# Four edits to the schedule of a one-core decoder block: first loads, two staging tiles, one unit's order of steps, one epilogue

## The chip, the cores and the metric

The kernel runs on one core of one Trainium2 chip. The metric is the device time of one execution, in microseconds (us). A core has a tensor engine for matmuls (PE; its loading of the standing operand is listed as PEld), a vector engine (DVE), a scalar engine (ACT), GpSimd (POOL) and a sync engine (SP). The engines run side by side, each takes its own instructions in order, and they wait for one another through semaphores. SP and POOL are used here mainly to issue transfers (DMAs) between DRAM and the on-chip memory.

## What is computed

The block takes x (256 tokens, 4096 channels, float32), normalises it, and projects it to 20480 channels. Half-width parts of that feed two branches; both branches go back to full width, are weighted by sigmoid gates and added, pass an output matrix, and the result is added to x and normalised again. Cut to what matters:

```
h    = rmsnorm(x, norm_w)
proj = h @ w_in                                   # (256, 20480)
u_p, z_p, u_c, b_c, c_c, z_c, g = split(proj)     # six parts of 2048, one of 8192
y_pool = pool(u_p, pool_w, pool_scale) * silu(z_p)
y_conv = b_c * conv3(c_c * u_c) * silu(z_c)
br     = [y_pool @ w_branch[0], y_conv @ w_branch[1]]
merged = sum over n of sigmoid(g[n] + gate_b[n]) * br[n]
out    = rmsnorm(x + merged @ w_out, final_norm_w)
```

## The kernel before

**Units and steps.** All the large products are cut into *units* of 1024 output columns for all 256 tokens. The units run in this order: `cu0, cc0, cz0, cb0, cu1, cc1, cz1, cb1` (the convolution branch, L583 to L620), `pz0, pu0, pz1, pu1` (pooling), eight gate units `g0_0, g1_0, ... g1_3`, then `b0_0, b1_0, b0_1, ... b1_3` (the branch products), and `o0` to `o3` (the output matrix). A unit is a row of *steps*; one step multiplies 256 channels of the left operand with a 256 x 1024 block of weights and adds into PSUM banks. A unit has 16 steps (branch units 8, whose left operand has 2048 channels).

**Two kinds of step.** Every float32 operand is split into a high and a low part in a reduced format, and three products of parts stand for one. A plain step, P, is 24 matmuls of 128x512. A Strassen step, S, is 21 matmuls (seven products of three) but needs sums of the weight blocks first: `sums`, `direct`, `t13` and `t24` (L264 to L287). ACT writes the high parts (`act`, L68) and DVE makes sums and low parts (`add` and `sub`, both L71), from the tile `raw`, where the weights land, to the tile `ring`, from which PE reads. Each S step also uses four PSUM banks called shared, in which the epilogue of the unit before does its transposes.

**What sets the order.** The program is written out in one static order by a small planner. `pump` (L1073) prepares weights up to AHEAD = 3 steps in front of PE, as far as the `ring` of 60 slots has room (a P step takes 16, an S step 28), and issues the next weight load as soon as one of NRAW = 3 slots of `raw` is prepared (L1076). `tick` (L1110) runs once per 6 matmuls: it takes one item from the epilogue's queue of the unit before, and calls `pop_fill`. In `after_group` (L1128) the emptying of finished PSUM banks comes first, then the ticks, then the limit is moved and `pump` runs. So an epilogue is a list of items, one per tick, in which `gap(n)` stands for n empty ticks. Where the S steps of a unit stand is given by a sequence: `seq_even` puts them at 2, 4, 6, 8, 10, 12, 14, `seq_turned` (L571, `spread_sequence(NS_X, 5)`) at 5, 7, 8, 10, 11, 12, 14. Unit `cu1` uses `seq_turned`, and so does `pz0`.

**Left operands.** The first 20 units use the parts of x, held in the tile `arena`. The branch units use y, kept in DRAM (`y_d`), and the output units use the merged result (`m_d`). When the last gate unit `g1_3` begins, `queue_fills` (L1147) lists all these operands in the order of their use as *fills*: eight for branch 0, eight for branch 1, two more for each branch's last unit (`y_last`, the same channels in the plain form, which go to the slots of the operands that they replace), and those of m. `pop_fill` (L837) looks at each tick at that list. At most one fill is done per PACE = 5 ticks: ACT and DVE split a staged operand into `arena`, if it was fetched at least LANDING = 6 ticks ago and its slot is free. Then, if one of the two staging tiles (`sa`, upper half, and `sb`) is empty, POOL fetches (`move`, L90) the next operand:

```
used = [f.st for f in fills if f.at is not None]
st = next((q for q in stages if not any(q is u for u in used)), None)
to_come = [f for f in fills if f.at is None and not isinstance(f, Direct) and f.ready()]
if st is not None and to_come:
    nxt = next((f for f in to_come if f.free()), None if used else to_come[0])
```

A fill whose slot is not free can thus be fetched when both stages are empty, and then keeps its stage until the slot is free. `ready` says whether y is there: for branch 0 always, for branch 1 from the start of `b0_0`. A step whose operand is not there yet forces a fill (L1188).

**The first steps.** The very first step is loaded in three pieces, the first 512 columns of each of two halves of the channels and then the other 512 columns, with x's first part in between (L1062 to L1066, SP). `par` (the convolution's taps and bias, 32 KB) is loaded at step 6 of the program by POOL, which has nothing before it and issues at once. While the first steps run, ACT squares x piece by piece (`square`, L949) and DVE adds; after the last piece one fold is left to do in halves, and at step 10 PE sums over the channels with ones (`sum_squares`, L960). The root mean square enters later, when a unit's sums are read out of PSUM by `evacuate` (L416, ACT, tile E or the unit's own target).

**The branch units' epilogue** (L721) in ticks, for branch 1: fetch the gate into E, 7 empty ticks, the product R = R * E, an empty tick, the sum R = R + Y with branch 0's part, 5 empty ticks, the transposes of R on PE (L466) with copies out, and the store to `m_d`.

Of the kernel before, what the change touches and what calls it, by code (L numbers as in the profile page):

```python
# [32 lines left out]
P = 128  # L33
T = 256
# [19 lines left out]


@with_exitstack
def hybrid_block(ctx: ExitStack, tc: tile.TileContext, x, x_t, norm_t, w_in, pool_w, pool_scale,
                 conv_t, gate_b, w_branch, w_out, final_norm_w, out):

# [166 lines left out]
    class Step:  # L226
# [95 lines left out]
        def groups(self):  # L322

            gs = []
            if self in steps[0:2]:

                for n in range(2):

                    order = ((0, 0), (1, 0), (0, 1), (1, 1), (2, 0), (2, 1)) if self is steps[0] and n == 0 else (
                        [(i, k) for i in range(3) for k in range(2)])  # L330
                    for i, k in order:
                            for t in range(2):
                                ah, al = self.op.standing(k, t)
                                h, l = self.h[n][:, k], self.l[n][:, k]
                                gs.append([("E", t, n), [((ah, h), (al, h), (ah, l))[i]], None])
                    gs[-1][2] = [(self.blocks[n], 8)]
            elif self.kind == "P":
                order = [(t, n) for n in self.halves for t in self.toks]
                if self.ending:
                    order = [(t, n) for t in self.toks for n in self.halves]  # L340
                for t, n in order:
                    mm = []
                    for k in range(2):
                        ah, al = self.op.standing(k, t)
                        h, l = self.h[n][:, k], self.l[n][:, k]
                        mm += [(ah, h), (ah, l), (al, h)]
                    gs.append([("E", t, n), mm, None])
                    if self.final and t == self.toks[-1]:
                        gs[-1][2] = [(self.blocks[n], 8)]
            elif self.kind == "S":  # L350
                prods = {"M1": (A11, self.dh, self.dl, 0, ("F", 0, 0)),
                         "N3": (Q3, self.dh, self.dl, 1, ("E", 0, 0)),
                         "M2": (A12, self.dh, self.dl, 2, ("E", 0, 1)),
                         "N5": (Q5, self.h13, self.l13, 0, ("F", 0, 1)),
                         "N7": (Q7, self.h13, self.l13, 1, ("F", 1, 0)),
                         "N6": (Q6, self.h24, self.l24, 0, ("F", 1, 1)),
                         "N4": (A22, self.h24, self.l24, 1, ("E", 1, 1))}
                order = ("N3", "M2", "N4", "M1", "N5", "N7", "N6") if self.closing else (
                    "M1", "N3", "M2", "N5", "N7", "N6", "N4")
# [127 lines left out]
    def gap(n):  # L487
        return [None] * n
# [94 lines left out]
    def conv_units(c, first=False):  # L583
        base = 2 * HALF + c * NU

        def c_epi(u):
            items = gap(1) + [lambda: mul(R, R, Y)] + gap(8)

            def taps(j):
                v, y = bankview(j), chan(Y)  # L590
                for i in range(2):
                    b = 2 * j + i
                    kb = 8 * c + b
                    act(y[:, b], v[:, i], AF.Identity, scale=par[:, 32 + kb:33 + kb], bias=par[:, 48 + kb:49 + kb])
                for i in range(2):
                    b = 2 * j + i
                    kb = 8 * c + b
                    for s in (1, 2):
                        col = 16 * (2 - s) + kb
                        stt(y[:, b, s:], v[:, i, 0:T - s], par[:, col:col + 1], y[:, b, s:], ALU.mult, ALU.add)  # L600

            for f in transposes(R, taps):
                items += [f, None]
            return items

        def gate(j):
            y = chan(Y)[:, 2 * j:2 * j + 2]
            mul(y, bankview(j), y)

        def z_epi(u):  # L610
            return sigmoid_mul() + [lambda: move(z_d[c], R)]

        def b_epi(u):
            return [lambda: move(E, z_d[c])] + gap(6) + [lambda: mul(R, R, E)] + gap(4) + transposes(R, gate) + [
                lambda: put(y_d[1, c], chan(Y))]

        in_unit(f"cu{c}", base, lambda u: [], seq=seq_0 if first else seq_turned, dst=Y)
        in_unit(f"cc{c}", base + 2 * HALF, c_epi, seq=seq_even if c else None)
        in_unit(f"cz{c}", base + 3 * HALF, z_epi)
        in_unit(f"cb{c}", base + HALF, b_epi, seq=seq_even)  # L620
# [99 lines left out]
    def branch_unit(n, c):  # L720
        def epi(u):  # L721
            if n == 0:
                return gap(2) + [lambda: mul(Y, R, Y)]
            items = [lambda: move(E, gates_d[n, c])] + gap(7)

            def copy(j):
                act(chan(Y)[:, 2 * j:2 * j + 2], bankview(j))
            return items + [lambda: mul(R, R, E), None, lambda: add(R, R, Y)] + gap(5) + pairs(
                transposes(R, copy)) + [
                lambda: c < 3 and put(m_d[c], chan(Y)), lambda: merged.update({c: now[0] + (STORED if c < 3 else 0)})]  # L730

        def src(i):
            return wbr[n, c, i]
        direct = c == 3 and n in DIRECT_LAST
        units.append(Unit(f"b{n}_{c}", src, seq_yp if direct else seq_y, y_last[n] if direct else y_ops[n], epi,
                          before=None if n else lambda: move(Y, gates_d[n, c])))
        return units[-1]
# [211 lines left out]
    def square(c):  # L949

        src = xc(2 * c, 2 * c + 2)
        if c == 0:
            act(sq, src, AF.Square)
        else:
            act(flat(V), src, AF.Square)
            add(sq, sq, flat(V))
        if c == 7:
            add(sq[:, 0:2 * T], sq[:, 0:2 * T], sq[:, 2 * T:])

    def sum_squares():  # L960
        for t in range(2):
            for k in range(2):
                pin(nc.tensor.matmul(sums_x[:, t:t + 1], sq[:, k * T + t * P:k * T + (t + 1) * P], ones[:, 0:1],
                                     start=k == 0, stop=k == 1))

    def diagonals():
        for t, q in enumerate((diag, std)):
# [67 lines left out]
    for i, c in squares.items():  # L1035
        after(i, square, c)
    before(6, load_x, 12, 16)
    before(6, move, par, conv_t)
    at(10, sum_squares)
    at(10, rstd)  # L1040
    at(10, diagonals)
# [14 lines left out]
    def issue_load(s):  # L1056
        i = s.load_index
        r = raw[:, i % NRAW]
        if s.kind == "M":
            load(r.rearrange("p (k n) -> p k n", k=4), s.src)  # L1060
        elif i == 0:
            q = r.rearrange("p (k n) -> p k n", k=2)  # L1062
            load(q[:, 0, 0:NH], s.src[:, 0, 0:NH])
            load_x(0, 1)
            load(q[:, 1, 0:NH], s.src[:, 1, 0:NH])
            load(q[:, :, NH:NU], s.src[:, :, NH:NU])  # L1066
        else:
            load(r.rearrange("p (k n) -> p k n", k=2), s.src)
        s.raw = r
# [77 lines left out]
    def queue_fills():  # L1147
# [3 lines left out]
            prev, owner[o.region] = owner[o.region], o  # L1151
            return freed(prev)

        def from_y(n, o, i):
            later(o, y_d[n, i // 4][:, i % 4].rearrange("p k t -> p (k t)"), place_of(o), lambda: n == 0 or units_done[0])

        def from_m(o, i):
            c = i // 4
# [9 lines left out]
                from_y(n, y_ops[n][i], i)  # L1168
        for n in DIRECT_LAST:
            for i in range(NP_Y, ny):  # L1170
                from_y(n, y_last[n][i], i)
        for i in order_of(seq_late):
            from_m(m_ops[i], i)

# [154 lines left out]
def _layout(i):  # L1329
# [3 lines left out]
    def by_step(w, pairs, units):  # L1333
# [4 lines left out]
        "x": i["x"],  # L1338
        "x_t": i["x"][0].T.reshape(D // T, 2, P, T).transpose(2, 0, 1, 3),
        "norm_t": i["norm_w"][0].reshape(-1, P).T,  # L1340
        "w_in": by_step(i["w_in"][0], D // T, -1),
        "pool_w": i["pool_w"][0].reshape(4, 4, P, NH).transpose(0, 2, 1, 3),
        "pool_scale": i["pool_scale"],
# [28 lines left out]
```

## Time and profile before

| | us |
|---|---|
| median of 3 runs | 2400.67 |
| lowest, highest | 2400.47, 2402.05 |
| the profiled execution's own time | 2400.08 |
| its span, from the first instruction to the last | 2398.4 |
| PE busy in it | 2380.3 |
| DVE busy | 2101.8 |
| ACT busy | 1351.6 |

The mean clock that TensorE was granted is 0.998 of full speed. A profile is of one execution, and its times count from its first instruction. In its timelines a row gives start, duration, engine, line of the kernel, operation, what it writes and reads, the count of instructions merged, and in brackets the idle time of the engine before it and what ended that idle time. In the groups by line, the numbers after the bar are the busy time, the mean duration in ns, and after the second bar the idle time before them. Where helpers record every operation, the line is the helper's (L68, L71, L83, L86, L90), and the tile's name tells which work it is. A stored copy of x's norm weights is named `par_n`; the matmuls of all steps are at L1122.

### The profile page before, as it was taken

How to read it: one execution, taken by the hardware profiler on the slowest of the kernel's cores; microseconds unless marked ns; L12 is line 12 of the kernel's file. 1: busy time of each engine (PE TensorE's matmuls, PEld its weight loads, DVE VectorE, ACT ScalarE, POOL GpSimd, SP SyncE). 2: the span in 40 equal slices, each digit the busy share in tenths (PEclk: the TensorE clock that was granted, in tenths of full speed). 3: DMA queues.
4: the chain of work that ended last, by engine and by line, in shares of the span. 5: the costliest groups of instructions: out<-in, count | busy, mean ns of one | idle time of the engine just before them, and what ended most of it. 6: DMA issues, size and time to landing. Idle time of an engine off the chain costs nothing.

```text
span 2398.4 us, 27788 instructions
## 1 busy us (share of the span) xinstructions
PE 2380.3 (99%) x10608; PEld 1970.6 (82%) x10608; DVE 2101.8 (88%) x2094; ACT 1351.6 (56%) x1392; POOL 61.2 (3%) x135
## 2 busy tenths in 40 slices
PE   9999999999999999999999999999999999999998
PEld 7888888888888888888888888888878888888886
DVE  8889989988989868968999899889888886799998
ACT  7555555555556555556555555555564555555564
POOL 0000000000000000000000000000000001000000
PEclk9999999999999999999999999999999999999999
DMA  8455564555566445545666566566666568556657
GB/s 334 167 202 196 224 244 179 211 202 202 212 242 228 187 180 224 219 176 221 236 237 233 214 224 222 212 242 232 254 242 236 214 255 291 207 204 246 249 216 272
DMA packets 79830, 538.73 MB, mean 225 GB/s; under 512 B 9152, under 2 KB 9152, under 8 KB 18512
## 3 DMA queue, kind: packets, MB, share of 16 engines
q1 hardware_dynamic: 68240, 484.47, 54.1%
q0 software_dynamic: 11024, 51.42, 6.3%
q8 instruction: 83, 1.36, 0.2%
q10 hardware_dynamic: 432, 1.07, 0.1%
q14 instruction: 51, 0.42, 0.0%
HBM read 511.75 MB, written 25.17 MB: 224 GB/s over the span
## 4 chain that ended last, share of the span: by engine, by line
PE 97%; DVE 1%; DMA 1%; issue 0%; ACT 0%; SPq 0%; DVEq 0%; ACTq 0%
PE sums L1122 77%; PE shared L1122 18%; PE shared L690 1%; PE shared L466 1%; DMA raw<-in_w_in_dram 1%; DVE ring L71 0%; DMA E<-gates_d 0%; DVE R L71 0%; ACT ring L68 0%; PE shared L669 0%; PE shared L670 0%; PE shared L672 0%; SPq L86 0%; DVE raw L71 0%; DVE V L71 0%
## 5 line engine op out<-in xcount | busy, mean ns | idle before, releaser
L1122 PE MATMUL sums<-ring,arena 128*128 128x512 f32 x8292 | 1942.3, 390 | 5.0 <-ACT arena L68 3.3
L1122 PEld LDWEIGHTS sums<-ring,arena 128*128 128x128 f32 x8292 | 1553.6, 188 | 328.3 <-ACT ring L68 2.5
L68 ACT ACTIVATE ring<-raw 128x1024 fp32r<-128x1024 f32 (+2 forms) x901 | 988.2, 1136 | 744.5 <-PE sums L1122 263.3
L71 DVE TENSOR_TENSOR ring<-raw,ring 128x1024 fp32r<-128x1024 f32 (+2 forms) x901 | 1162.3, 1322 | 216.6 <-ACT ring L68 184.7
L1122 PE MATMUL shared<-ring,arena 128*128 128x512 f32 x1968 | 497.1, 389 | 0.0
L1122 PEld LDWEIGHTS shared<-ring,arena 128*128 128x128 f32 x1968 | 369.5, 188 | 76.6
L68 ACT ACTIVATE ring<-V 128x1024 fp32r<-128x1024 f32 x164 | 173.2, 1056 | 115.4 <-DVE V L71 76.3
L71 DVE TENSOR_TENSOR V<-raw 128x1024 f32<-128x1024 f32 x164 | 199.9, 1219 | 1.4 <-DMA raw<-in_w_out_dram 1.4
L71 DVE TENSOR_TENSOR ring<-V,ring 128x1024 fp32r<-128x1024 f32 x164 | 199.9, 1219 | 0.3 <-ACT ring L68 0.2
L71 DVE TENSOR_TENSOR raw<-raw 128x512 f32<-128x512 f32 x164 | 113.5, 692 | 5.7
L71 DVE TENSOR_TENSOR raw<-V,raw 128x512 f32<-128x512 f32 x164 | 113.4, 691 | 5.1
L71 DVE TENSOR_TENSOR R<-R,E 128x1024 f32<-128x1024 f32 (+1 forms) x55 | 95.1, 1745 | 4.7 <-DMA E<-gates_d 3.7
L68 ACT ACTIVATE E<-sums,rin 128x512 f32<-128x512 f32 (+1 forms) x57 | 44.7, 826 | 30.6 <-PE sums L1122 30.3
L71 DVE TENSOR_TENSOR R<-R,shared 128x512 f32<-128x512 f32 x84 | 57.4, 683 | 1.1
L68 ACT ACTIVATE arena<-sa 128x512 fp32r<-128x512 f32 (+2 forms) x41 | 22.4, 567 | 49.1 <-DVE sa L71 44.0
L71 DVE TENSOR_TENSOR R<-R,Y 128x1024 f32<-128x1024 f32 (+1 forms) x28 | 40.4, 1447 | 0.0
L71 DVE TENSOR_TENSOR arena<-sa,arena 128x512 fp32r<-128x512 f32 (+2 forms) x41 | 24.5, 616 | 11.9 <-ACT arena L68 11.9
L466 PEld LDWEIGHTS shared<-ident,R 128*128 128x128 f32 x160 | 19.3, 140 | 5.4 <-DVE R L71 1.3
L466 PE MATMUL shared<-ident,R 128*128 128x128 f32 x160 | 22.7, 273 | 0.9 <-DVE R L71 0.9
L68 ACT ACTIVATE R<-R 128x2048 f32<-128x2048 f32 x8 | 15.3, 1909 | 14.5 <-DVE R L71 14.5
L690 PE MATMUL shared<-ring 128*128 128x512 f32 x96 | 22.1, 389 | 0.0
L690 PEld LDWEIGHTS shared<-ring 128*128 128x128 f32 x96 | 18.0, 188 | 3.7
(132 smaller groups left out, 402.0 us busy)
## 6 DMA issues: line engine op xcount, KB each, us to landing
raw<-in_w_in_dram SPq DMA_DIRECT2D x319, 1024.0 KB, 4.9
raw<-in_w_branch_dram SPq DMA_DIRECT2D x64, 1024.0 KB, 5.3
raw<-in_w_out_dram SPq DMA_DIRECT2D x64, 1024.0 KB, 4.9
gates_d<-R POOLq DMA_DIRECT2D x8, 1024.0 KB, 5.2
raw<-in_pool_w_dram SPq DMA_DIRECT2D x4, 1024.0 KB, 4.8
Y<-in_gate_b_dram POOLq DMA_DIRECT2D x8, 512.0 KB, 6.9
Y<-gates_d POOLq DMA_DIRECT2D x4, 1024.0 KB, 8.9
E<-gates_d POOLq DMA_DIRECT2D x4, 1024.0 KB, 5.5
```

The costliest lines, as they stand in the source:

```text
L68: return pin(nc.scalar.activation(dst, src, func, **kw))
L71: return pin(nc.vector.tensor_tensor(out=dst, in0=a, in1=b, op=op))
L466: pin(nc.tensor.transpose(shared(j)[:, i * T + t * P:i * T + (t + 1) * P], src[:, t, c:c + P], ident))
L690: pin(nc.tensor.matmul(o, a[:, k, ts], b[:, k], start=(k, i) == (0, 0), stop=(k, i) == (3, 2)))
L1122: pin(nc.tensor.matmul(ps, lhs, rhs, start=n == 0, stop=n == u.total[b] - 1))
```

## The change

Six places are changed.

1. The first step's weights come from an extra input, `w_first`, which holds the same 256 x 1024 block as four pieces of 128 x 512, each contiguous in DRAM. The three loads stay, with the same bytes and targets.
2. `par` is loaded through SP and not through POOL, at the same place of the program.
3. After the last square, DVE folds the sums twice and not once, down to one column per token, and PE's sum over the channels takes two matmuls and not four.
4. `cu1` takes `spread_sequence(NS_X, 4)`: its S steps stand at 4, 6, 7, 9, 11, 12, 14.
5. In branch 1's epilogue the product moves one tick later, to the tick just before the sum. The length of the list is the same.
6. The two extra fills of each branch's last unit count as ready only when all sixteen first operands of both branches have been filled.

```
-            load(q[:, 0, 0:NH], s.src[:, 0, 0:NH])
+            load(q[:, 0, 0:NH], w_first[0, 0])
             load_x(0, 1)
-            load(q[:, 1, 0:NH], s.src[:, 1, 0:NH])
-            load(q[:, :, NH:NU], s.src[:, :, NH:NU])
+            load(q[:, 1, 0:NH], w_first[0, 1])
+            load(q[:, :, NH:NU], w_first[1].rearrange("k p n -> p k n"))
...
+        "w_first": i["w_in"][0][:T, 2 * HALF:2 * HALF + NU].reshape(2, P, 2, NH).transpose(2, 0, 1, 3),
...
-    before(6, move, par, conv_t)
+    before(6, load, par, conv_t)
...
         if c == 7:
-            add(sq[:, 0:2 * T], sq[:, 0:2 * T], sq[:, 2 * T:])
+            for n in (2 * T, T):
+                add(sq[:, 0:n], sq[:, 0:n], sq[:, n:2 * n])
...
         for t in range(2):
-            for k in range(2):
-                pin(nc.tensor.matmul(sums_x[:, t:t + 1], sq[:, k * T + t * P:k * T + (t + 1) * P], ones[:, 0:1],
-                                     start=k == 0, stop=k == 1))
+            pin(nc.tensor.matmul(sums_x[:, t:t + 1], sq[:, t * P:(t + 1) * P], ones[:, 0:1], start=True, stop=True))
...
-        in_unit(f"cu{c}", base, lambda u: [], seq=seq_0 if first else seq_turned, dst=Y)
+        in_unit(f"cu{c}", base, lambda u: [], seq=seq_0 if first else spread_sequence(NS_X, 4), dst=Y)
...
-            items = [lambda: move(E, gates_d[n, c])] + gap(7)
+            items = [lambda: move(E, gates_d[n, c])] + gap(8)
...
-            return items + [lambda: mul(R, R, E), None, lambda: add(R, R, Y)] + gap(5) + pairs(
+            return items + [lambda: mul(R, R, E), lambda: add(R, R, Y)] + gap(5) + pairs(
...
-        def from_y(n, o, i):
-            later(o, y_d[n, i // 4][:, i % 4].rearrange("p k t -> p (k t)"), place_of(o), lambda: n == 0 or units_done[0])
+        def from_y(n, o, i, ready=None):
+            later(o, y_d[n, i // 4][:, i % 4].rearrange("p k t -> p (k t)"), place_of(o),
+                  ready or (lambda: n == 0 or units_done[0]))
...
-                from_y(n, y_last[n][i], i)
+                from_y(n, y_last[n][i], i, lambda: all(o.ready for q in y_ops for o in q))
```

More of the change, by code (lines that the diff above doesn't have):

```diff
@@ L56, in hybrid_block @@
 @with_exitstack
-def hybrid_block(ctx: ExitStack, tc: tile.TileContext, x, x_t, norm_t, w_in, pool_w, pool_scale,
+def hybrid_block(ctx: ExitStack, tc: tile.TileContext, x, x_t, norm_t, w_first, w_in, pool_w, pool_scale,
                  conv_t, gate_b, w_branch, w_out, final_norm_w, out):
@@ L331, in groups @@
                     for i, k in order:
[L332 to L335, printed above, removed]
+                        for t in range(2):
+                            ah, al = self.op.standing(k, t)
+                            h, l = self.h[n][:, k], self.l[n][:, k]
+                            gs.append([("E", t, n), [((ah, h), (al, h), (ah, l))[i]], None])
                     gs[-1][2] = [(self.blocks[n], 8)]
```

## The prediction

> **What bounds the kernel now.** I read the page first: TensorE's share, then who it waited for, then its timeline, since only a hole in TensorE's row can be worth time here.
>
> ```profile
> span 2398.4 us, 27788 instructions
> ...
> PE 2380.3 (99%) x10608; PEld 1970.6 (82%) x10608; DVE 2101.8 (88%) x2094; ACT 1351.6 (56%) x1392; POOL 61.2 (3%) x135
> ...
> L1122 PE MATMUL sums<-ring,arena 128*128 128x512 f32 x8292 | 1942.3, 390 | 5.0 <-ACT arena L68 3.3
> ```
>
> PE is busy for 2380.3 of 2398.4 us. Matmuls are not removed by this change except four tiny ones, so the most that it can give is what PE spends not multiplying. The waits of PE list all of it that lies between its first and last instruction:
>
> ```profile
> PE sums L1122 <- ACT arena L68: 3.3, 2, 2.0
> PE sums L1122 <- ACT E L68: 1.3, 1, 1.3
> PE shared L927 <- DVE rout L932: 1.1, 1, 1.1
> PE shared L466 <- DVE R L71: 0.9, 1, 0.9
> PE sums L1122 <- ACT ring L68: 0.3, 1, 0.3
> ```
>
> Six holes, 6.9 us together (the columns are total, times, longest); the rest of the difference lies behind the last matmul and isn't touched. The timeline of PE gives each hole its place, in brackets at a row's end:
>
> ```profile
> 6.01 5.75 PE L1122 MATMUL sums<-ring,arena 128*128 128x512 f32 x24 [1.28 <-ACT arena L68]
> 12.10 49.30 PE L1122 MATMUL sums<-ring,arena 128*128 128x512 f32 x216 [0.34 <-ACT ring L68]
> 61.24 0.95 PE L963 MATMUL shared<-ones,sa 128*128 128x1 f32 x8
> 62.04 5.75 PE L1122 MATMUL sums<-ring,arena 128*128 128x512 f32 x24
> ...
> 423.50 6.28 PE L1122 MATMUL sums<-ring,arena 128*128 128x512 f32 x27
> 431.12 11.34 PE L1122 MATMUL sums<-ring,arena 128*128 128x512 f32 x48 [1.34 <-ACT E L68]
> ...
> 1788.21 2.62 PE L1122 MATMUL sums<-ring,arena 128*128 128x512 f32 x9 [2.00 <-ACT arena L68]
> ...
> 1817.60 1.09 PE L466 MATMUL shared<-ident,R 128*128 128x128 f32 x8 [0.93 <-DVE R L71]
> ```
>
> Two corrections turn idle into lost time. A 128x512 matmul lasts 390 ns (the page's row of the costliest group) and 27 of them take 6.28, so one starts every (6.28 - 0.39) / 26 = 0.227 us, which is 0.16 before its predecessor ends: each hole costs its idle time plus 0.16. And the first ones after a hole are slower: 48 in a row should take 47 x 0.227 + 0.39 = 11.04, the row at 431.12 says 11.34 (0.30 more); nine should take 2.20, the row at 1788.21 says 2.62 (0.42 more). So the four holes are worth, in order, 0.34 + 0.16 = **0.50** at 12.10; 1.34 + 0.16 + 0.30 = **1.80** at 431; 2.00 + 0.16 + 0.42 = **2.58** at 1788; 0.93 + 0.16 = **1.09** at 1817.
>
> **The change, part by part.**
>
> *Sum of squares (step 10).* Eight instructions at L963 (four matmuls, two passes each) hold PE from 61.24 to 62.04, 0.80 us. Two matmuls remain: half, **0.40 us** gained. Added is one fold on DVE, half the size of the present one:
>
> ```profile
> 48.21 0.69 DVE L71 TENSOR_TENSOR sa<-sa 128x512 f32<-128x512 f32 x1
> ```
>
> At most 0.69 us more DVE at 49 us, 12 us ahead of its use, under the 216 matmuls from 12.10 that run without a hole. Cost 0; without that cover, at most 0.69.
>
> *Start.* The chain of waits over the first 70 us goes through SP's issues to one transfer:
>
> ```profile
> 3.52 7.45 DMA raw<-in_w_in_dram
> ```
>
> Timelines of SP, DVE and ACT (start, duration, work, [idle before]):
>
> ```profile
> 0.81 0.39 SPq L86 DMA_DIRECT2D raw<-in_w_in_dram  x1
> ...
> 5.51 0.35 DVE L993 TENSOR_SCALAR arena<-R,par_n 128x256 fp32r<-128x256 f32 x1 [4.43 <-DMA R<-in_x_t_dram]
> ...
> 10.99 2.01 ACT L68 ACTIVATE ring<-raw 128x1024 fp32r<-128x1024 f32 x2 [1.52 <-DMA raw<-in_w_in_dram]
> ```
>
> Two stretches of the windows view (the last column is GB/s):
>
> ```profile
> 2.00:4.00 2.00, 2.00 (x11) 1.45 (x10) 0.00 (x0) 0.73 (x2) 0.81 (x17) 1.00 0.65 158
> ...
> 8.00:10.00 2.00, 2.00 (x11) 1.55 (x9) 1.30 (x2) 1.47 (x3) 0.00 (x0) 1.00 1.00 422
> ```
>
> The second step's weights land at 3.52 + 7.45 = 10.97 and its matmuls start at 12.10; the first step's start at 6.01 hangs on x, queued on SP behind the first weights. The core reads 158 GB/s at 2 to 4 us and 422 at 8 to 10. Had the first stretch run at the later rate, the same bytes would be in (422 - 158) x 2 / 422 = 1.25 us earlier; that is the most that a better order in memory can bring. The edit moves no byte less for the weights: rows of 2 KB per partition remain, only their neighbours in DRAM change. What leaves these microseconds for certain is par's load (32 KB from POOL), worth 32 / 422 = 0.08 us at that rate. Its new place on SP is behind x's last load, where one more issue stands under the hole-free 216 matmuls; it is read only by the second unit's epilogue. The trace does not show the new pattern. Bounds: 0.39 us lost (each later issue behind a first one of twice its 0.39) to 1.25 gained; I take **0.30**, between the 0.08 that is certain and the 0.50 at 12.10, beyond which PE's own start would have to move with x.
>
> A rule speaks against this part. The Trainium skill's DMA: Bandwidth & Descriptors (Latency and other measured facts, HBM row pitch) has reads slowed by a power-of-two pitch only from megabytes up: 207 GB/s at 512 KiB against 214 at full rate; here the pitch is 8 KB, so by it the runs bring nothing. The slow stretch at 158 GB/s neither confirms nor denies that. By that rule this term would be 0.08 and the result 0.2 us later.
>
> *One unit's S steps apart (cu1, which ends at 423.50 + 6.28 = 429.8 us).* The hole at 431 is the next unit's first matmul waiting until ScalarE has emptied the sums. ScalarE was late because it stood at an earlier instruction, for a transfer (the chain of waits, then ACT's timeline):
>
> ```profile
> 422.12 6.35 DMA raw<-in_w_in_dram
> ```
>
> ```profile
> 428.58 1.49 ACT L68 ACTIVATE ring<-raw 128x1536 fp32r<-128x1536 f32 x1 [0.62 <-DMA raw<-in_w_in_dram]
> 429.97 1.09 ACT L68 ACTIVATE E<-sums,rin 128x1024 f32<-128x1024 f32 x1
> ```
>
> That transfer was issued at 422.12, the moment DVE had finished the step that held the slot. So DVE's lateness is the cause. Two lines views of DVE, 350 to 380 us and 380 to 424 us (busy, mean ns | idle before), then four rows of its timeline:
>
> ```profile
> L71 DVE TENSOR_TENSOR ring<-raw,ring 128x1024 fp32r<-128x1024 f32 (+1 forms) x9 | 11.9, 1339 | 5.1 <-ACT ring L68 4.1 <-PE sums L1122 1.0
> ...
> L71 DVE TENSOR_TENSOR ring<-raw,ring 128x1024 fp32r<-128x1024 f32 (+1 forms) x19 | 25.2, 1362 | 0.3
> ```
>
> ```profile
> 376.99 1.76 DVE L71 TENSOR_TENSOR ring<-raw,ring 128x1536 fp32r<-128x1536 f32 x1 [1.81 <-ACT ring L68]
> ...
> 390.71 1.22 DVE L71 TENSOR_TENSOR V<-raw 128x1024 f32<-128x1024 f32 x1
> ...
> 397.40 1.22 DVE L71 TENSOR_TENSOR V<-raw 128x1024 f32<-128x1024 f32 x1
> ...
> 413.07 1.22 DVE L71 TENSOR_TENSOR V<-raw 128x1024 f32<-128x1024 f32 x1
> ```
>
> DVE idles 5.1 us before 380 and 0.3 in the 44 us after. One S step costs it 397.40 - 390.71 = 6.7 us, against 21 x 0.227 = 4.8 on PE; 413.07 - 397.40 = 15.7 is two S and one P, so a P costs 2.3. The S steps now stand at 5, 7, 8, 10, 11, 12, 14; they will stand at 4, 6, 7, 9, 11, 12, 14. The first four come one step earlier, so DVE does 6.7 - 2.3 = 4.4 us of its work earlier, where it idles; from the wait at 376.99 alone 1.8 us can be filled. The evacuation must come 1.34 + 0.16 = 1.5 us earlier, so even the smaller figure is just enough: **1.80 gained**. At worst nothing is filled and the hole stays (0), or an earlier S step comes late by as much as DVE would gain and takes the 1.80 back inside the unit; the 5.1 us idle in front of it speak against that.
>
> *Two stages for the second branch (b0_0 and b1_0).* The 2.00 us hole is b1_0's last S step waiting for its left operand, the last of eight fills. POOL's timeline, and the view of the operands' tile from 1713 to 1790 us:
>
> ```profile
> 1689.14 0.54 POOL L90 DMA_DIRECT2D sa<-y_d  x1 [13.74 <-DVE arena L71]
> ...
> 1690.20 0.54 POOL L90 DMA_DIRECT2D sb<-y_d  x1
> ```
>
> ```profile
> L68 ACT ACTIVATE arena<-sb x8: 507/615/633, 1715.8 to 1788.1; 128x512 fp32r<-128x512 f32 x6, 128x384 fp32r<-128x384 f32 x2
> ```
>
> The sa stage is taken at 1689 by an operand of a later unit, and all eight fills go through sb. One stage takes a tick to fetch and six to land, 7 ticks of six matmuls (1.36 us) a fill; with two stages the limit is PACE, 5 ticks. From 1715.8 seven more fills then end near 1715.8 + 7 x 6.8 = 1763 us, over 20 us ahead of the need. The DVE work that comes along earlier (three of the eight fills) goes from a stretch without idle time to one with 9.7 us of it (lines of DVE, 1713 to 1763 and 1763 to 1789):
>
> ```profile
> L71 DVE TENSOR_TENSOR ring<-raw,ring 128x1024 fp32r<-128x1024 f32 (+1 forms) x18 | 22.6, 1281 | 9.7 <-ACT ring L68 9.7
> ...
> L71 DVE TENSOR_TENSOR ring<-raw,ring 128x1024 fp32r<-128x1024 f32 (+1 forms) x10 | 12.8, 1325 | 0.1
> ```
>
> **2.58 gained**; 0 if DVE were late anyway. POOL issues the same transfers; the later unit's fetch falls behind the branch's gate transfers on its queue, and its own fill has to wait for a slot that unit b0_2 releases, long after.
>
> *Gate product next to its sum (b1_0's epilogue).* PE's transposes wait for the sum R:
>
> ```profile
> 1807.66 2.29 DVE L71 TENSOR_TENSOR R<-R,E 128x2048 f32<-128x2048 f32 x1 [2.45 <-DMA E<-gates_d]
> ...
> 1815.26 2.28 DVE L71 TENSOR_TENSOR R<-R,Y 128x2048 f32<-128x2048 f32 x1
> ```
>
> DVE stands 2.45 us at the product until the gate lands, and between product and sum it does 1815.26 - 1807.66 - 2.29 = 5.3 us of an S step's preparation. That preparation is let in by the pump right after the tick that now carries the product; with the product one tick later, what one pump lets in runs ahead of it, in the wait: at least V<-raw, 1.22 us by the row at 390.71, and 1.09 are needed: **1.09 gained**. The gate's fetch follows the unit's end on PE, so the working holds when the hole at 1788 goes. If the preparation stayed behind, 0.
>
> **Sum.** 0.40 + 0.30 + 1.80 + 2.58 + 1.09 = 6.17 us. The profiled execution took 2400.08, so it would take 2393.9. The median of the runs is 2400.67, 0.6 above; I predict medians: **2394.5**.
>
> **Rivals,** from the same base.
> 1. The hole at 431 stays, since ring space, released by PE, sets the pace and not the order (for it: 1.0 of the 5.1 us idle ended on PE itself; against it: 0.3 us idle afterwards): 2394.5 + 1.80 = 2396.3. Chance 0.13.
> 2. The second stage doesn't do what it says: DVE's backlog makes the last fill late, as the 0.1 us idle before it would allow; against it, the fill now sits last in that backlog. 2394.5 + 2.58 = 2397.1. Chance 0.12.
> 3. The preparation stays between product and sum: 2395.6. Chance 0.12.
> 4. Slower. The ring of 60 slots wraps at other places after cu1's new order, and stays shifted for the 2000 us behind it. Each of the twelve later units with seven S steps could then end in a hole like the one at 431, 1.80 each. From the fourth on it outweighs 6.17; seven make 2394.5 + 12.6 = 2407.1. Against it: today none of these twelve ends in one, by the list of PE's waits. Chance 0.06.
>
> **Chances.** Forecast 0.55 (2393.5 to 2395.2 by the start's bounds), two rivals at once 0.02. The range 2393.2 to 2397.4 takes in the forecast and rivals 1 to 3. About 0.2% (4.8 us, below 2395.87) is what a measurement can tell from no change: faster 0.64 (forecast, two thirds of rival 3, a little of rival 1), slower 0.05, same 0.31.
>
> **What would show it.** Right: PE's waits list keeps only the start's two; no bracket near 430, 1786, 1814; y_d fills alternate sa and sb after 1690; x4 at L963. Wrong: a new bracket in cu1 or at any unit's end, or DVE idle still standing at R<-R,E in b1_0.

## The result, and the profile after

| us | before | after |
|---|---|---|
| median | 2401.18 (2400.17 to 2402.05, 8 runs) | 2394.14 (2393.40 to 2394.63, 8 runs) |
| the profiled execution's own time | 2400.08 | 2393.45 |
| its span | 2398.4 | 2391.7 |

The ratio is 0.9971, with a 95% interval of 0.9960 to 0.9981. The forecast of 2394.5 is 0.4 too late. The median fell by 7.04, where the prediction had 6.17; its base of 2400.67, from three runs, lay 0.51 below the median of the eight. Helpers stand one line later in the changed kernel (L69 for L68, L72 for L71, L87 for L86, L91 for L90); the matmuls of the steps are still at L1122.

The page first, then all that PE still waits for (total, times, longest):

```profile
span 2391.7 us, 27786 instructions
...
PE 2379.3 (99%) x10604; PEld 1971.1 (82%) x10604; DVE 2101.4 (88%) x2095; ACT 1351.9 (57%) x1392; POOL 60.6 (3%) x134
```

```profile
PE shared L928 <- DVE rout L933: 1.1, 1, 1.1
PE sums L1122 <- ACT arena L69: 0.3, 1, 0.3
```

Of six holes two are left, both in the first 5 us. PE's timeline shows the four places of the prediction without a bracket: step 10's sum, the ends of `cu1` and `b1_0`, and the transposes.

```profile
5.05 11.13 PE L1122 MATMUL sums<-ring,arena 128*128 128x512 f32 x43 [0.33 <-ACT arena L69]
...
60.67 0.50 PE L964 MATMUL shared<-ones,sa 128*128 128x1 f32 x4
...
422.49 13.76 PE L1122 MATMUL sums<-ring,arena 128*128 128x512 f32 x60
...
1777.13 8.32 PE L1122 MATMUL sums<-ring,arena 128*128 128x512 f32 x36
...
1811.13 1.03 PE L467 MATMUL shared<-ident,R 128*128 128x128 f32 x8
```

Every matmul of the steps has the same number in both traces, so the time can be followed: the start of the n-th after, less its start before. This shift is -0.96 at the first matmul, -0.53 when the second step starts (12.10 to 11.57), -0.57 up to 61 us, -1.01 behind the sum of squares, -2.81 behind the end of `cu1`, -5.39 behind the end of `b1_0`, -6.55 behind its transposes, and -6.6 at the end. The steps are -0.57, -0.44, -1.80, -2.58 and -1.16; the prediction had 0.30, 0.40, 1.80, 2.58 and 1.09. Nothing was lost anywhere else.

Why the holes went is seen on the other engines. At the end of `cu1` ScalarE now empties the sums, for which it waits on PE itself, ahead of the S step's high part, for whose transfer it stood before:

```profile
426.09 1.12 ACT L69 ACTIVATE E<-sums,rin 128x1024 f32<-128x1024 f32 x1 [3.22 <-PE sums L1122]
427.10 1.48 ACT L69 ACTIVATE ring<-raw 128x1536 fp32r<-128x1536 f32 x1
```

DVE's backlog went the way of the working: 1.8 us idle between 350 and 380 us where there were 5.1, and 2.4 between 380 and 424 where there were 0.3 (the first groups of the two views).

```profile
L72 DVE TENSOR_TENSOR ring<-raw,ring 128x1024 fp32r<-128x1024 f32 (+1 forms) x9 | 12.6, 1399 | 1.8 <-ACT ring L69 1.5
...
L72 DVE TENSOR_TENSOR ring<-raw,ring 128x1024 fp32r<-128x1024 f32 (+1 forms) x21 | 26.9, 1322 | 2.4 <-PE sums L1122 1.5 <-ACT ring L69 0.6
```

The operands' tile between 1700 and 1800 us shows two stages at work, the last fill 19 us earlier than before (1769 for 1788; the working had 1763):

```profile
L69 ACT ACTIVATE arena<-sa x6: 612/615/633, 1713.0 to 1768.6; 128x512 fp32r<-128x512 f32 x6
L69 ACT ACTIVATE arena<-sb x4: 509/564/617, 1719.2 to 1769.1; 128x512 fp32r<-128x512 f32 x2, 128x384 fp32r<-128x384 f32 x2
```

And DVE has no idle time at the gate's product. It first does the S step's preparation, from `V<-raw` on:

```profile
1799.84 1.22 DVE L72 TENSOR_TENSOR V<-raw 128x1024 f32<-128x1024 f32 x1
...
1803.49 0.69 DVE L72 TENSOR_TENSOR raw<-raw 128x512 f32<-128x512 f32 x1
1804.10 2.28 DVE L72 TENSOR_TENSOR R<-R,E 128x2048 f32<-128x2048 f32 x1
...
1807.43 2.28 DVE L72 TENSOR_TENSOR R<-R,Y 128x2048 f32<-128x2048 f32 x1
```

One comparison of two executions can't say which edit brought which step, and some terms hang on when a transfer landed in these two. So each edit was undone alone.

### The profile page after: what moved, and what is told of

The parts are those of the page before. It is cut to its first block, busy times and chain, and to the rows that moved or that the text cites. A ratio compares the mean times of both kernels' runs of the same rounds, so it can differ in the third digit from the quotient of the medians.

```text
span 2391.7 us, 27786 instructions
## 1 busy us (share of the span) xinstructions
PE 2379.3 (99%) x10604; PEld 1971.1 (82%) x10604; DVE 2101.4 (88%) x2095; ACT 1351.9 (57%) x1392; POOL 60.6 (3%) x134
## 3 DMA queue, kind: packets, MB, share of 16 engines
q10 hardware_dynamic: 432, 1.07, 0.1%
## 4 chain that ended last, share of the span: by engine, by line
PE 99%; DVE 0%; DMA 0%; ACT 0%; issue 0%; DVEq 0%; SPq 0%; ACTq 0%
PE sums L1122 79%; PE shared L1122 19%; PE shared L691 1%; PE shared L467 1%; DMA R<-in_x_t_dram 0%; PE shared L670 0%; PE shared L671 0%; PE shared L673 0%; PE shared L672 0%; DVE raw L1308 0%; DVE E L84 0%; ACT V L69 0%; ACT arena L69 0%; DVE raw L1304 0%; PE shared L972 0%
## 5 line engine op out<-in xcount | busy, mean ns | idle before, releaser
L1122 PE MATMUL sums<-ring,arena 128*128 128x512 f32 x8292 | 1941.7, 390 | 0.3 <-ACT arena L69 0.3
L1122 PEld LDWEIGHTS sums<-ring,arena 128*128 128x128 f32 x8292 | 1554.5, 188 | 322.5 <-ACT ring L69 1.2
L69 ACT ACTIVATE ring<-raw 128x1024 fp32r<-128x1024 f32 (+2 forms) x901 | 988.5, 1136 | 736.3 <-PE sums L1122 264.0
L72 DVE TENSOR_TENSOR ring<-raw,ring 128x1024 fp32r<-128x1024 f32 (+2 forms) x901 | 1162.0, 1321 | 216.3 <-ACT ring L69 184.2
L1122 PE MATMUL shared<-ring,arena 128*128 128x512 f32 x1968 | 497.2, 389 | 0.0
L1122 PEld LDWEIGHTS shared<-ring,arena 128*128 128x128 f32 x1968 | 369.4, 188 | 76.6
L69 ACT ACTIVATE ring<-V 128x1024 fp32r<-128x1024 f32 x164 | 173.2, 1056 | 109.4 <-DVE V L72 75.3
L72 DVE TENSOR_TENSOR V<-raw 128x1024 f32<-128x1024 f32 x164 | 199.7, 1217 | 0.6 <-DMA raw<-in_w_out_dram 0.5
L72 DVE TENSOR_TENSOR ring<-V,ring 128x1024 fp32r<-128x1024 f32 x164 | 199.8, 1218 | 0.3 <-ACT ring L69 0.2
L72 DVE TENSOR_TENSOR raw<-raw 128x512 f32<-128x512 f32 x164 | 113.5, 692 | 5.7
L72 DVE TENSOR_TENSOR raw<-V,raw 128x512 f32<-128x512 f32 x164 | 113.3, 691 | 5.0
L72 DVE TENSOR_TENSOR R<-R,E 128x1024 f32<-128x1024 f32 (+1 forms) x55 | 95.0, 1744 | 1.9 <-DMA E<-gates_d 1.0
L69 ACT ACTIVATE E<-sums,rin 128x512 f32<-128x512 f32 (+1 forms) x57 | 44.8, 828 | 34.9 <-PE sums L1122 34.6
L72 DVE TENSOR_TENSOR R<-R,shared 128x512 f32<-128x512 f32 x84 | 57.3, 682 | 1.1
L69 ACT ACTIVATE arena<-sa 128x512 fp32r<-128x512 f32 (+2 forms) x45 | 24.9, 572 | 53.9 <-DVE sa L72 49.0
L72 DVE TENSOR_TENSOR R<-R,Y 128x1024 f32<-128x1024 f32 (+1 forms) x28 | 40.3, 1446 | 0.0
L72 DVE TENSOR_TENSOR arena<-sa,arena 128x512 fp32r<-128x512 f32 (+2 forms) x45 | 27.2, 621 | 11.7 <-ACT arena L69 11.7
L69 ACT ACTIVATE R<-R 128x2048 f32<-128x2048 f32 x8 | 15.3, 1911 | 14.5 <-DVE R L72 14.5
```

Source lines behind the costliest of these rows:

```text
L69: return pin(nc.scalar.activation(dst, src, func, **kw))
L72: return pin(nc.vector.tensor_tensor(out=dst, in0=a, in1=b, op=op))
L1122: pin(nc.tensor.matmul(ps, lhs, rhs, start=n == 0, stop=n == u.total[b] - 1))
```

## The experiments

If nothing else is said, a kernel is the changed one with the edit shown, and its median is to be held against 2394.14. The kernel before ran beside them with medians of 2400.77 to 2401.11, and beside the changed kernel with 2401.18: the common level moved by up to 0.41, so a difference of that size says nothing by itself. A trace shows one execution; those of experiments 6, 9 and 10 are of the longest of the eleven.

**1. `cu1` with its old order.**

```
-        ... seq=seq_0 if first else spread_sequence(NS_X, 4), dst=Y)
+        ... seq=seq_0 if first else seq_turned, dst=Y)
```

> The changed kernel with cu1's old order of steps (S at 5, 7, 8, 10, 11, 12, 14); all else as changed. Theory A (DVE's work came too late in this unit): the hole of 1.34 us of PE behind an ACT E wait stands again at cu1's end, all other holes stay away, PE's later work comes 1.8 us later than in the changed kernel, the time is about 2396.0 us. Rival B (what removed it was another edit, since everything in front of it moved by 1 us): no hole there, about 2394.1 us.

2396.11 (ratio to before 0.9980, 0.9971 to 0.9989), 1.97 slower than the changed kernel. The hole is back, and its cause too, ScalarE at a transfer (waits of PE, then ACT's timeline):

```profile
PE sums L1122 <- ACT E L69: 1.3, 1, 1.3
```

```profile
428.48 1.49 ACT L69 ACTIVATE ring<-raw 128x1536 fp32r<-128x1536 f32 x1 [1.34 <-DMA raw<-in_w_in_dram]
429.87 1.09 ACT L69 ACTIVATE E<-sums,rin 128x1024 f32<-128x1024 f32 x1
```

The shift gains nothing at `cu1` (-0.07 to -0.11 against before); the term of 1.80 is that of this edit.

**2. `cu1` turned the other way.** `spread_sequence(NS_X, 6)` in the same place.

> The changed kernel with cu1's S steps moved the other way, to 6, 7, 9, 10, 11, 13, 14; the same instructions otherwise. Theory A (each S step that comes later moves 4.4 us of DVE's work behind the stretch where DVE idles): a hole at cu1's end larger than with the old order, 3 to 6 us of lost time, about 2397 to 2400 us. Rival B (the hole comes from where the ring's slots happen to wrap, not from when DVE has its work): a hole of another size, 1.8 us or less, or none, 2394 to 2396 us.

2398.57 (0.9990, 0.9981 to 0.9999), 4.4 slower. The hole grows to 2.7 us, and ahead of the emptying ScalarE now waits until DVE itself is done (PE's and ACT's timelines):

```profile
432.11 8.17 PE L1122 MATMUL sums<-ring,arena 128*128 128x512 f32 x27 [2.72 <-ACT E L69]
```

```profile
429.57 1.48 ACT L69 ACTIVATE ring<-raw 128x1536 fp32r<-128x1536 f32 x1 [1.04 <-DVE ring L72]
```

DVE's idle time between 350 and 380 us (first group of the view) is 1.8 us in the changed kernel, 5.1 in experiment 1 and 6.8 here: it grows with the hole, so the place of the S steps sets it. But the shift loses 2.97 against before, whose hole of 1.34 cost 1.80: together 4.77, where a hole of 2.72 with 0.16 and 0.30 makes 3.18. The missing 1.6 us stands in the windows, in the column ahead of the DMA share, the granted clock:

```profile
432.00:434.00 2.00, 1.89 (x7) 1.42 (x8) 1.97 (x2) 2.00 (x4) 0.00 (x0) 0.91 0.80 336
434.00:436.00 2.00, 2.00 (x6) 1.52 (x6) 2.00 (x4) 1.21 (x2) 0.00 (x0) 0.50 0.00 0
436.00:438.00 2.00, 2.00 (x8) 1.64 (x7) 2.00 (x3) 1.06 (x1) 0.00 (x0) 0.74 0.00 0
```

About 1.5 us after the hole's end TensorE fell to half its clock, for about 3.4 us by these windows, with matmuls 0.43 apart and not 0.227. A hole can cost more than its length.

**3. The old readiness of the second branch's fills.**

```
-                from_y(n, y_last[n][i], i, lambda: all(o.ready for q in y_ops for o in q))
+                from_y(n, y_last[n][i], i)
```

> The changed kernel with the old readiness of the two extra fills, so that one of them sits in the sa stage while branch 1's operands are filled. Theory A: all of branch 1's fills go through sb, the last S step of b1_0 waits again for its operand, 2.6 us lost there; the transposes behind it do not wait, since the product's new place holds by itself: about 2396.7 us. Rival B (the transposes' hole went only because the last fill no longer stood in DVE's queue): that hole returns as well, 3.7 us lost, about 2397.9 us.

2396.05 (0.9981, 0.9972 to 0.9990), 1.91 slower. All eight fills go through `sb` again (the operands' tile from 1700 to 1800 us), and a hole for the last one is back, but a shorter one (waits of PE, then its timeline):

```profile
L69 ACT ACTIVATE arena<-sb x8: 507/615/634, 1713.9 to 1785.2; 128x512 fp32r<-128x512 f32 x6, 128x384 fp32r<-128x384 f32 x2
```

```profile
PE sums L1122 <- ACT arena L69: 1.2, 2, 1.0
```

```profile
1785.32 2.61 PE L1122 MATMUL sums<-ring,arena 128*128 128x512 f32 x9 [1.01 <-ACT arena L69]
...
1813.61 1.04 PE L467 MATMUL shared<-ident,R 128*128 128x128 f32 x8
```

The hole costs 1.6 with its tail, not 2.58. Three of the eleven runs took 2397.3 to 2399.0, the other eight 2394.9 to 2396.3: such a gap is of the size of the half-clock stretch in experiment 2, but no trace of those three exists.

**4. The gate's product back in its old tick.**

```
-            items = [lambda: move(E, gates_d[n, c])] + gap(8)
+            items = [lambda: move(E, gates_d[n, c])] + gap(7)
...
-            return items + [lambda: mul(R, R, E), lambda: add(R, R, Y)] + gap(5) + pairs(
+            return items + [lambda: mul(R, R, E), None, lambda: add(R, R, Y)] + gap(5) + pairs(
```

> The changed kernel with the old epilogue of branch 1 (product one tick earlier). Theory A: DVE stands about 2 us at the product R,E of b1_0 waiting for the gate, does the S step's preparation behind it, and the transposes wait about 0.9 us again: 1.1 us lost, about 2395.2 us. Rival B (with the fills out of the way DVE is early enough and the edit was needless): no hole at the transposes, about 2394.1 us.

2393.82 (0.9971, 0.9961 to 0.9982): nothing is lost, and the transposes wait for nothing. DVE does wait at the product, with the preparation behind it, as before:

```profile
1801.43 2.29 DVE L72 TENSOR_TENSOR R<-R,E 128x2048 f32<-128x2048 f32 x1 [1.23 <-DMA E<-gates_d]
1803.64 1.22 DVE L72 TENSOR_TENSOR V<-raw 128x1024 f32<-128x1024 f32 x1
...
1809.04 2.29 DVE L72 TENSOR_TENSOR R<-R,Y 128x2048 f32<-128x2048 f32 x1
```

The sum ends at 11.33 past 1800, the transposes start at 11.48: it is just in time. The wait of 1.23 was 2.45 in the trace of before, because the gate took 6.38 us from its issue at 1801.18 to its landing there, and 5.16 here.

**5. Experiments 3 and 4 together.** After 3 and 4 it looked as if either edit alone kept the transposes from waiting.

> The changed kernel with both the old readiness of the second branch's fills and the old place of the gate product. Theory A (either of the two edits alone keeps the transposes from waiting, since both move the product against the sum): both holes of b1_0 return, 1.0 to 2.0 us on an arena fill near 1785 and about 0.9 on DVE's R near 1811; the cumulative gain over before, 2.8 just ahead of b1_0, stays there or falls by under 0.5 in it, and the median is 2 to 4 us above the changed kernel, 2396 to 2398. Rival B (the transposes' hole went for another reason, such as the gate's transfer landing sooner by chance): only the arena hole returns, and the median is that of the old readiness alone, about 2396.

2396.14 (0.9983, 0.9974 to 0.9992), as experiment 3 alone. The arena hole is 1.46 us here, the transposes again start without a bracket, and the product waits 1.19 for a gate that took 5.12. So rival B holds: it was the landing. With the product in its old tick four traces show transfers of 6.38, 5.16, 5.12 and 5.23 us (before, experiments 4, 5 and 9), and a hole only with 6.38. With the new tick ten traces show 5.08 to 6.58 and no hole at this place. In the trace of experiment 1 the gate took 6.58 and the product started 1.6 us after its landing; in that of experiment 12 it took 6.49, and the product started 1.7 us after. By this the edit would be worth about 1.1 us in an execution with a late gate and nothing in the others. That is an estimate: the trace of before is the only one with a late gate and the old tick. Three of the eleven runs took 2397.1 to 2397.8, as in experiment 3; whether by a late gate or in another way, no trace shows.

**6. The first step's weights from w_in again.**

```
-            load(q[:, 0, 0:NH], w_first[0, 0])
+            load(q[:, 0, 0:NH], s.src[:, 0, 0:NH])
```

and the other two pieces likewise.

> The changed kernel with the first step's weights read from the large tensor as before (rows of 2 KB, 8 KB apart); par stays on SP. In the changed kernel PE's first step starts at 5.05 us and its second at 11.57, against 6.01 and 12.10 before. Theory A (the runs in DRAM made the first transfers land earlier): first start near 5.9, second step at 12.0, 0.45 us lost. Rival B (par's transfer from POOL was what held the first transfers up): first start near 5.1, second near 11.6, nothing lost. Rival C (the start differs by as much from execution to execution): any start between the two, not tied to the edit.

2396.06 (0.9980, 0.9971 to 0.9988), 1.92 slower: six times the 0.30 of the prediction. PE starts at 7.00 and then runs slowly:

```profile
7.00 9.18 PE L1122 MATMUL sums<-ring,arena 128*128 128x512 f32 x28 [2.29 <-ACT arena L69]
```

28 matmuls at 0.227 would take 6.5; the first ones start 0.43 us apart until 12.3.

**7. `par` by POOL again,** `before(6, move, par, conv_t)`.

> The changed kernel with par loaded by POOL again at the start, the first weights in runs as changed. Theory A (par is worth its 32 KB, 0.08 us): first start near 5.1 us, second step near 11.65, about 0.1 us lost. Rival B (par was what held the first transfers up): first start near 5.9, second at 12.0, 0.45 us lost. Rival C: not tied to the edit.

2393.82 (0.9971, 0.9959 to 0.9982): nothing lost.

**8. Both edits of the start undone.**

> The changed kernel with both edits of the start undone (weights from the large tensor, par by POOL). Theories A and B: first start near 6.0 us and second step near 12.1, as before the change, 0.5 us lost, about 2394.7 us. Rival C (the start differs from execution to execution): a start near 5.05 can be seen here as well.

2395.54 (0.9978, 0.9970 to 0.9987), 1.40 slower. The first matmul is at 6.01 as in the trace of before, but the row is another:

```profile
6.01 10.29 PE L1122 MATMUL sums<-ring,arena 128*128 128x512 f32 x35 [1.29 <-ACT arena L69]
```

Its first matmuls start 0.43 us apart until 10.4 us; those of the kernel before, from the same 6.01, started 0.23 apart from the second on. The second step starts at 13.64 and not at 12.10, and neither here nor in experiment 6 does it wait for its weights. ScalarE had written their first high part by 13.2 here and by 13.9 there, 1.1 us after they landed, and PE was still at the slow first step. By these figures the half rate cost the two executions about 0.4 and 1.2 us, an estimate. So the profiled execution of before had a good start, and a trace pair hides most of what w_first brings.

**9. w_first alone, on the kernel before.**

> The kernel before with the first step's weights from w_first and nothing else. Theory C (w_first is worth more than the 0.30 predicted, because PE's idle stretch ahead of the first step shrinks from 1.3 to 0.3 us and with it the half-rate stretch): 1.2 to 1.9 us below the kernel before, about 2399.5; first matmul near 5.0. Prediction's own working: 0.22 to 0.30 us, 2400.8. The rule on power-of-two pitches: nothing.

2399.70 against 2400.77, 1.07 less; but the ratio is 0.9998, with an interval of 0.9989 to 1.0006 that holds both theories. It settles nothing on the start. Its trace has the old hole at the end of `b1_0`, and behind it what experiment 2 showed (PE's timeline, then windows):

```profile
1788.69 3.62 PE L1122 MATMUL sums<-ring,arena 128*128 128x512 f32 x9 [1.91 <-ACT arena L68]
1792.11 3.53 PE L1122 MATMUL shared<-ring,arena 128*128 128x512 f32 x12
```

```profile
1790.00:1792.00 2.00, 2.00 (x6) 1.61 (x5) 1.97 (x2) 1.88 (x3) 0.00 (x0) 0.50 0.69 291
1792.00:1794.00 2.00, 2.00 (x7) 1.52 (x7) 0.39 (x1) 1.43 (x4) 0.00 (x0) 0.65 0.34 53
```

The hole of 1.91 costs 1.52 more than that of 2.00 in the trace of before, where the nine matmuls took 2.62. The transposes of this execution don't wait either.

**10. More warm-up matmuls under the old start:** experiment 8 with `WARM_1` at 11 and not 6.

> The changed kernel with the old start (weights of the first step from w_in, par by POOL), but with 11 instead of 6 warm-up matmuls behind the first ten, so that PE is busy until 5.86 us and stands idle for about 0.2 instead of 1.3 ahead of the first real matmul at 6.0. Theory C (what the old start costs is mostly PE's half rate: PE's idle stretch ahead of x lets its clock fall back, in many executions): no more than 5 matmuls 0.43 apart, full rate before 8 us, and the median falls from 2395.5 to about 2394.4, within 0.7 of the changed kernel. Rival D (the cost is the transfers alone): median stays near 2395.5, and the slow matmuls last until 10 us as before.

2395.49 (0.9980, 0.9971 to 0.9989), no change from 8: the median of rival D, though its slow matmuls are not there. In its trace PE runs at full rate from the first matmul on, x itself lands later, and the second step still starts at 14.79, after its weights, which were issued at 3.53 and took 10.12 (PE's timeline, then the chain of waits):

```profile
6.56 3.01 PE L1122 MATMUL sums<-ring,arena 128*128 128x512 f32 x12 [1.33 <-ACT arena L69]
11.19 3.06 PE L1122 MATMUL sums<-ring,arena 128*128 128x512 f32 x12 [1.62 <-ACT ring L69]
14.79 1.45 PE L1122 MATMUL sums<-ring,arena 128*128 128x512 f32 x5 [0.54 <-ACT ring L69]
```

```profile
3.53 10.12 DMA raw<-in_w_in_dram
```

By this median the clock is not what the old start costs in the main; the transfers are. But PE still stood idle for 1.33 us ahead of x in this execution, and not for the 0.2 that was expected.

**11. More warm-up matmuls in the changed kernel,** `WARM_1` at 8.

> The changed kernel with 8 instead of 6 warm-up matmuls behind the first ten: PE busy until about 5.18 us, the first real matmul at 5.05 to 5.2 with no idle time ahead of it. If the 0.3 us that PE idles there still delays its full rate, the slow matmuls of 5 to 6.5 us shrink and the median falls by 0.2 to 0.5 us (2393.5). If an idle stretch that short does not count, the first matmul is 0.1 us later and the time the same within 0.2 us.

2394.56 (0.9977, 0.9968 to 0.9986): no gain, though its trace has the first matmul at 5.10 and full rate from there. In that execution the transposes of a later unit, at 1985 us, waited 1.08 for the sum, because DVE stood for 4.33 us at an output operand's fill ahead of the product: such holes still come and go in the changed kernel.

**12. Four matmuls and one fold for the sum of squares.**

> The changed kernel with four matmuls for the sum of squares and one fold on DVE. Theory A: eight instructions at the sum of squares hold PE 0.8 us instead of 0.4; all later work 0.4 us later, about 2394.6 us. Rival B (the second fold on DVE delayed something that gives it back): less than 0.2 us lost. The start of this run, the same as in the changed kernel, tells how much the start differs between executions.

2394.42 (0.9972, 0.9962 to 0.9983), 0.28 slower; in the trace eight instructions again hold PE for 0.80 us.

No version ran better than the changed kernel by more than the scatter: 4 and 7, which undo one edit each, are 0.32 lower with overlapping ranges.

## Why the prediction was right, and where it wasn't

| us | predicted | the two traces | edit undone, median |
|---|---|---|---|
| sum of squares | 0.40 | 0.44 | 0.28 |
| start | 0.30 | 0.57 | 1.92 (w_first), -0.32 (par), 1.40 (both) |
| order of cu1 | 1.80 | 1.80 | 1.97 |
| two stages | 2.58 | 2.58 | 1.91 |
| gate's product | 1.09 | 1.16 | -0.32 |
| sum | 6.17 | 6.55 | |

*The number was met in part by luck.* Undone alone, the edits cost 0.28, 1.40 (both of the start together), 1.97, 1.91 and -0.32, 5.24 us in all, while the median fell by 7.04. The 1.8 between them belong to no single edit. A part may be that `b1_0`'s hole is longer in the traces with `cu1` in its old order (below), another the half-clock stretches behind the longer holes of some executions; neither is shown.

*Read off rightly.* The method, to list PE's holes, take each with its overlap of 0.16 and its slow tail, and ask which edit takes its cause away, gave the steps of the trace within 0.1 us for all but the start. The order of `cu1` and the sum of squares stand by mechanism and size. For `cu1` the experiments show the chain as it was worked out: with the S steps later, ScalarE stands at a late transfer with the emptying behind it; with them one step later still it waits for DVE itself, and the hole doubles. Rivals 1, 2 and 4 fell: no hole at 431, two stages at work, no new hole at any later unit's end in the trace. Rival 3 fell too: the preparation did move ahead of the product.

*The start was mis-sized.* The step that failed is "between the 0.08 that is certain and the 0.50 at 12.10, beyond which PE's own start would have to move with x". PE's own start did move, from 6.01 to 5.05, because x lands at 4.45 and not at 5.40 behind the first weights. And 12.10 was not the old start's usual place. In the four traces with the old source the second step's weights land at 10.96, 12.11, 12.83 and 13.65, and the step starts at 12.10, 13.64, 15.12 and 14.79; in the ten with w_first they land between 10.44 and 11.54, and it starts between 11.57 and 12.67. Of the four, the starts at 12.10 and 14.79 waited for the weights; those at 13.64 and 15.12 waited for a first step that began late and ran slowly. I took the earliest of a wide spread for the rule. By medians the old source costs the changed kernel 1.35 to 1.92 us (experiments 6, 8 and 10), even more than the upper bound of 1.25; on the kernel before w_first brings 1.07, with an interval that holds 0.30 as well. The 0.08 "that is certain" for `par` is too small to be seen: experiment 7 lost nothing. Taken together, the early stretches show faster reads with w_first (windows of the changed kernel; 158, 371 and 390 GB/s in the trace of before):

```profile
2.00:4.00 2.00, 2.00 (x11) 1.45 (x10) 0.00 (x0) 0.96 (x3) 0.05 (x2) 1.00 0.84 296
4.00:6.00 2.00, 1.67 (x6) 1.01 (x5) 1.42 (x4) 1.22 (x3) 0.00 (x0) 1.00 0.94 337
6.00:8.00 2.00, 2.00 (x8) 1.60 (x7) 1.04 (x2) 1.29 (x3) 0.00 (x0) 1.00 1.08 421
```

In experiment 8 the same three stretches moved 203, 285 and 282. A part is SP's: the third load of the weights and the load of x behind it are issued in less time (0.43 and 0.47 us for 0.65 and 0.59), so that the second step's weights are issued at 3.18 and not at 3.52. w_first differs from the old source in two ways: its pieces are contiguous, and it is a tensor of its own at another place in DRAM. No run separates the two, so which of them makes the reads faster stays open, and so does why the old start spreads so widely.

The Trainium skill's DMA: Bandwidth & Descriptors (Latency and other measured facts, HBM row pitch) gives no pitch below 512 KiB, and the prediction read from it that the new order in memory brings nothing, 0.08 for the whole start. The start brought more: the first weights, with a pitch of 8 KB in the old source, landed at 4.43 to 4.75 in four traces, and from w_first at 3.57 to 3.81 in ten. Whether the pitch did it isn't shown, so the row itself is neither confirmed nor refuted.

*The gate's product was put down to a wait that isn't always there.* "DVE stands 2.45 us at the product until the gate lands" was true of one execution. The preparation did move ahead of the product as predicted, but only in three of the fourteen traces did the gate take over 6.3 us; with the 5.1 to 5.3 of the others in the old tick there is no hole to remove. The 1.16 in the trace pair is the luck of the trace of before; the edit can serve as a cover against a late landing, of which no run shows the gain.

*The two stages were over-sized:* undone, the hole is 1.0 or 1.5 us (experiments 3 and 5), with `cu1` in its old order 1.9 or 2.0 (experiment 9 and before). The ring's slots stand differently after `cu1`'s new order, which could set DVE's backlog at the last fill; that is argued and not shown.

So errors of the sum go against each other: what the start brought beyond its 0.30 on one side, and on the other the gate's 1.09 that is there only now and then and the 0.67 by which the two stages alone fell short of 2.58.

## What to carry to other kernels

In a kernel whose main engine is busy for 99%, the engine's list of waits is the list of what can be won: price each hole with the pipeline overlap and the slow instructions behind it, and follow the releaser back to the engine that was late. But look at more than one execution before a hole that ends on a DMA is booked as a gain: a hole that comes from order (`cu1`) stood in all three traces with the old order, one that hangs on a landing (the gate, the first loads) is there in some executions and not in others. And undo every edit alone, since a sum that fits can hold terms that are wrong in opposite directions; and add up what the edits cost alone, since the whole can be worth more.

## What the runs showed of the hardware

*A hole of 1.9 us can halve TensorE's clock.* After the hole of 1.91 in experiment 9 the granted clock was 0.50 and 0.65 in the next stretches, and after that of 2.72 in experiment 2 0.50 and 0.74; after the hole of 2.00 in the trace of before the matmuls went on 0.23 apart from the fourth on. The fall came 1.3 and 1.5 us after the matmuls had resumed and lasted about 3.4 us in both, and behind the start no other matmuls of the steps stand 0.43 apart in the fourteen traces. The price was about 1.5 us more, in some executions. The Trainium skill's TensorE: Matmul & The Clock Gate (What's actually happening) tells of a free-running window of about 3.4 us and of a fall to half rate after an idle window; that each stretch lasted about 3.4 us, and that a hole of much the same length does or doesn't bring it, agree with the free-running window, but the holes here were shorter than one.

*The start of the kernel varies in the same way,* and there the column of the granted clock doesn't show it. In the trace of experiment 8 it is 1.00 from 2 to 10 us, while matmuls start 0.43 apart until 10.4 us; in the ten traces with w_first the last such pair began at 6.5 us or earlier, or there was none. Early in a program the spacing of the matmuls is the better clock.
